# A hybrid decoder block on one core: an unnormalised first input projection, and two request orders changed

## The chip, the cores and the metric

The kernel runs on 1 core of one Trainium2 chip. The metric is the device time of one execution in microseconds (us). All engines named here belong to that core: PE (TensorE) multiplies matrices, DVE (VectorE), ACT (ScalarE) and POOL (GpSimd) work element by element, SP (SyncE) issues DMAs here.

## The reference

One decoder layer on 2048 tokens of width 1024, in f32. What matters of it here:

```
h = rmsnorm(x, norm_mix_gain)                 # x * rsqrt(mean(x*x) + eps) * gain
z = h @ w_in                                  # 1024 -> 3072, split into nine streams
y = [rglru(z...), hgrn2(z...), shortconv(z...)]     # three causal token mixers
x = x + y @ w_out
x = x + (silu(g) * u) @ w_down                # g, u = split(causal_conv3(rmsnorm(x) @ w_up))
x = x + sigmoid(x @ w_gate) * (p @ w_proj)
return rmsnorm(x, final_norm_gain)
```

The norm of a token is one number, 1/rms, which multiplies every feature of that token. So the product of a row of x (with the gain) and w_in, multiplied by 1/rms afterwards, is the same as the product of the normed row and w_in.

## The kernel before, in words

**Layout.** Features lie on the 128 partitions, tokens on the free axis. The 2048 tokens are worked in two halves (`hf`) of 1024, each in two chunks (`c`) of 512. A product in f32 is three matmuls (`mm3`, lines 265 to 267): both operands are split into a rounded part hi and a rest lo (`split`: hi by ACT, line 258; lo by a subtraction on DVE, line 259), and hi·hi, hi·lo and lo·hi are added in PSUM.

**Stages of a half.** The input projection (24 units of 128 columns in the order `IN_UNITS`; a unit is 2 chunks × 8 feature blocks × 3 = 48 matmuls of 128x512 into a PSUM tile `pz`) runs woven with the mixers; then come the output projection, the MLP (22 pairs of a gate block and an up block), the gate of the layer embedding, and the final norm of the half.

**Who sets the order.** The program is one long instruction stream in Python, and a scheduler gives each engine a fixed queue. On PE the mixers' small matmuls stand among the input projection's: a generator `G` of the projection's matmul triples is advanced by `fill(n)` (n triples, each one feature block of one chunk), `fill_to` and `weave`. When a unit is done, `evac` (line 559) calls the stream's function (`hg_f`, `hg_q`, `rg_u`, ...), which reads `pz` from PSUM. There are two tiles `pz`; a third unit can begin when the first one's readers are done. Weights are loaded by SP into three raw buffers `wr` and split in the order of a list (`w_upto`, `w_get` with a lookahead).

**The start.** SP loads x of chunk 0 (four tiles `xl` of 512 KB), constants, the first weights and x of chunk 1. The norm of a chunk (`Norm`) is 8 squares on ACT (line 306), 7 additions on DVE or POOL (line 308), 4 small matmuls `pm` (line 316), a few tiny steps on DVE and ACT (lines 319 to 325) and a broadcast `pr` by matmul (line 332). `h_apply` (line 416) then makes the normed h: `hx` = x * gain * 1/rms (line 420, DVE, reading `pr`) and a split. Only then can the first `pz` matmul run. The first two units are interleaved by chunk: unit 1 chunk 0, unit 2 chunk 0, unit 1 chunk 1, unit 2 chunk 1.

**The MLP's first pairs.** Pairs 0 and 1 go through `up_first`, later ones through `up(j)` in a scheme of seven quarter products (X[1] to X[7] are sums and differences of h, made in steps of the generator `h2`; the weights' sums `s` are made on DVE, lines 166 to 177, and split into `wt`). In `up(2)`, the third pair, PE first runs `pa` = X[1] times weight (1, hf, 2). Behind it stand the products into `pb`, `pa`, `pc`, and then the down projection `pdn` of pairs 0 and 1, which reads the activations `ahi` and `alo` that `gu_split` makes after `g_silu` and `gu_mul`. During the first half's MLP `stats_steps` loads x of the second half in pieces `xs` and squares and adds them, one piece per pair.

Of the kernel before, what the change touches and what calls it, by code (L numbers as in the profile page):

```python
# [9 lines left out]
F32 = mybir.dt.float32  # L10
F32R = mybir.dt.float32r
# [9 lines left out]
CH = 512  # L21
# [27 lines left out]
def trunk(ctx, tc, xT, pT, w_in, w_out, w_up, w_down, w_pp, w_pg, wr_bd, wi_bd, vecs, consts, masks, out):  # L49
# [34 lines left out]
    def ps2(name="ps2"):  # L84
        return mm.tile([P, TH], F32, tag="mm", name=nm(name))
# [4 lines left out]
    def cks(c):  # L90
        return slice(c * CH, (c + 1) * CH)
# [187 lines left out]
    def run(g):  # L279
        for _ in g:  # L280
            pass
# [134 lines left out]
    def h_apply(dst, xs, gain, pr, pool=()):  # L416

        for k in range(KD):
# [2 lines left out]
            dst[k] = split_chunk(s, "h", nc.gpsimd if k in pool else None)  # L421
            yield

    def stats_stream(hf, c):
        n = Norm()
        for k in range(KD):
            s = t2("xs")
            nc.gpsimd.dma_start(s, xT[k, :, hf * TH + c * CH : hf * TH + (c + 1) * CH])
            n.add(s)
        n.rstd()  # L430
        return n
# [8 lines left out]
    def x_load(xs, hf, c, eng):  # L440

        t0 = hf * TH + c * CH
        for k in range(0, KD, 2):
            t = t4("xl")
            eng.dma_start(t.rearrange("p (k t) -> p k t", k=2), xT[k : k + 2, :, t0 : t0 + CH].rearrange("k p t -> p k t"))
            xs += [t[:, :CH], t[:, CH:]]

    x_load(x0[0], 0, 0, nc.sync)
    nc.sync.dma_start(kt, consts[:, :KBLK])
    w_upto(1)  # L450
    nc.sync.dma_start(vt, vecs)
    w_upto(2)
    x_load(x0[1], 0, 1, nc.sync)
    norms = [Norm(), Norm()]
    for k in range(KD):
        norms[0].add(x0[0][k])
    norms[0].rstd()
    pr = norms[0].bcast()
    for k in range(KD):
        norms[1].add(x0[1][k], nc.gpsimd, True)  # L460
    run(h_apply(h[0], x0[0], "g1", pr))
    nc.vector.memset(hcar, 0.0)
    nc.vector.memset(scar, 0.0)

    for hf in range(NH):
# [91 lines left out]
        EVAC = [(9, hg_f), (6, hg_q), (12, hg_v), (15, hg_g), (0, rg_u), (3, rg_g), (20, sc_c), (22, sc_v), (18, sc_b)]  # L557

        def evac(m, ps):
            for b0, fn in EVAC:  # L560
                if b0 <= m < b0 + (3 if b0 < 18 else 2):
                    fn(m - b0, ps)

        done = [0]

        def gemm():

            ws, pss = [w_get("in", hf, m) for m in IN_UNITS[:2]], [ps2("pz"), ps2("pz")]
            for c in range(NC):
                for i in range(2):  # L570
                    yield from proj_gen(pss[i][:, cks(c)], ws[i], h[c])
                    if c == NC - 1:
                        evac(IN_UNITS[i], pss[i])
                        done[0] += 1
            for m in IN_UNITS[2:]:
                w, ps = w_get("in", hf, m), ps2("pz")
                for c in range(NC):
                    yield from proj_gen(ps[:, cks(c)], w, h[c])
                evac(m, ps)
                done[0] += 1  # L580

        G = gemm()
# [142 lines left out]
                ys[c][k] = split_chunk(y[k][:, cks(c)], "ys")  # L725

        if first:
            fill(6)
            norms[1].rstd()
            fill(5)  # L730
            run(h_apply(h[1], x0[1], "g1", norms[1].bcast(), (1, 3, 5)))
            with tc.issue_after(last_split[0].ins), tc.issue_after(last_split[1].ins):
                derived()
            t = t4("blk")[:, :P]
            nc.scalar.dma_start(t, consts[:, KBLK:])
            ACT(blk, t, AF.Copy)
# [137 lines left out]
        def gu_split(j):  # L874
            hi, lo = t4("ahi", F32R), t4("alo", F32R)
            split(hi, lo, zs[j, "g"])
            acts[j] = (hi, lo)

        def up_first():

            pairs = range(FIRST)
            w = {}
            sums0 = [[ps1(name="pa"), ps1(name="pa")], None]
            for j in pairs:
                zs[j, 0], zs[j, 1] = ftile("zg"), ftile("zu")
            for j in pairs:
                if j:
                    t = ps2("pbc")
                    sums0[j] = [t[:, C0], t[:, C1]]
                for i in range(2):  # L890
                    w[j, i] = w_get("f", hf, j, i)
                    prod(sums0[j][i], w[j, i], X[1], True, False)
                    ACT(zs[j, i][:, C1], sums0[j][i], AF.Copy)
                    if j == 0 and i == 0:
                        norms[1].rstd()
                    if j == 0 and i == 1:
                        h2 = h2_second(norms[1].bcast())
                        next(h2)
            for j in pairs:
                for i in range(2):  # L900
                    w[j, 2 + i] = w_get("f", hf, j, 2 + i, ahead=min(2, 3 - 2 * j - i))
                    prod(sums0[j][i], w[j, 2 + i], X[2], False, True)
                    ACT(zs[j, i][:, C0], sums0[j][i], AF.Copy)
                next(h2)

            sums1 = []
            for j in pairs:
                t = ps2("pbc")
                sums1.append([t[:, C0], t[:, C1]])
                for i in range(2):  # L910
                    prod(sums1[j][i], w[j, i], X[5], True, False)
            next(h2)
            for j in pairs:
                for i in range(2):
                    prod(sums1[j][i], w[j, 2 + i], X[3], False, True)
                    TT(zs[j, i][:, C1], zs[j, i][:, C1], sums1[j][i], op=ADD)
                if j == 0:
                    g_conv(0)
                    u_conv(0)
                    g_silu(0)  # L920
                    gu_mul(0)
                    gu_split(0)
                    run(h2)
                else:
                    g_conv(1)

        banks = {}

# [5 lines left out]
        def up(j):  # L934
            A, B = ps1(name="pa"), ps1(name="pb")
            banks[j] = A
            zg, zu = zs[j, 0], zs[j, 1] = ftile("zg"), ftile("zu")
            prod(A, w_mlp(1, hf, j), X[1], True, False)
            ACT(zg[:, C0], A, AF.Copy)
            if j % 2 == 0 or j == NJ - 1:  # L940
                g_silu(j - 1)
            prod(B, w_mlp(5, hf, j), X[5], True, False)
            ACT(zu[:, C1], B, AF.Copy)
            if j > FIRST:
                last_prod(j - 1)
            u_conv(j - 1)
            prod(A, w_mlp(6, hf, j), X[6], False, False)
            ACT(zg[:, C1], A, AF.Copy)
            gu_mul(j - 1)
            Cc = ps1(name="pc")  # L950
            prod(Cc, w_mlp(2, hf, j), X[2], True, True)
            TT(zg[:, C0], zg[:, C0], Cc, op=ADD)
            gu_split(j - 1)
            prod(B, w_mlp(3, hf, j), X[3], False, True)
            TT(zg[:, C1], zg[:, C1], B, op=ADD)
            prod(A, w_mlp(7, hf, j), X[7], False, False)
            TT(zu[:, C1], zu[:, C1], A, op=ADD)
            g_conv(j)
# [61 lines left out]
        stats = iter(()) if last else stats_steps()  # L1020
        for j in range(FIRST, NJ):
            up(j)
            next(stats, None)
            if j % 2 == 0 and j < NJ - 2:
                down_pair(j // 2 - 1, lambda: g_silu(j))
        run(stats)
# [167 lines left out]
```

## Time and profile before

| | |
|---|---|
| median of 3 runs | 2505.47 us (2500.73 to 2506.73) |
| the profiled execution's own time | 2501.25 us |
| its span | 2499.5 us |
| PE busy | 2423.0 us (97%) |
| DVE busy | 1578.3 us (63%) |
| ACT busy | 1253.3 us (50%) |
| POOL busy | 192.2 us (8%) |

The span is the traced part of the profiled execution. Busy time is the time in which an engine worked on data. An engine at 97% can only lose the time in which it waits or runs at a lower clock, or get fewer instructions.

### The profile page before, as it was taken

The page shows a single profiled execution, that of the slowest core. Times are in us where ns is not written, and L with a number is a line of the kernel's source. Part 1 is how long each engine was busy: PE and PEld are TensorE (multiplying, and loading weights), DVE is VectorE, ACT ScalarE, POOL GpSimd, SP SyncE. Part 2 cuts the span into 40 slices and gives each one's busy share as a digit, 9 for nine tenths or more (in the row PEclk, how much of TensorE's full clock was granted, in tenths as well). Part 3 has the DMA queues.
Part 4 walks back from the last instruction along what each step waited for, and adds up shares of the span by engine and source line. Part 5 has one row for each costly group of instructions (what it writes and reads, how often), then busy time and mean ns, then how long its engine had stood idle before and what let it go on. Part 6 is the DMA issues. An engine that isn't in the chain of part 4 may idle for free.

```text
span 2499.5 us, 33974 instructions
## 1 busy us (share of the span) xinstructions
PE 2423.0 (97%) x13660; PEld 1991.4 (80%) x13660; DVE 1578.3 (63%) x2396; ACT 1253.3 (50%) x1696; POOL 192.2 (8%) x240
## 2 busy tenths in 40 slices
PE   5999999889999999999999999998999999999998
PEld 4787788668888888888887787886888888888888
DVE  6566555585555565587565756567666666666856
ACT  5244873355555555545343457734555555555443
POOL 2000001001111111100110000010111111111000
PEclk9999999999999999999999999999999999999999
DMA  3101115435555555533431111251555555555442
GB/s 138 44 28 38 46 54 175 132 95 137 136 135 131 137 136 141 128 137 118 139 105 35 36 35 55 80 189 43 127 132 138 130 127 127 132 134 122 144 144 93
DMA packets 116542, 271.84 MB, mean 109 GB/s; under 512 B 11552, under 2 KB 39840, under 8 KB 116384
## 3 DMA queue, kind: packets, MB, share of 16 engines
q0 software_dynamic: 29056, 104.87, 19.9%
q1 hardware_dynamic: 86320, 163.78, 19.9%
q8 instruction: 107, 1.75, 0.3%
q10 hardware_dynamic: 1008, 1.02, 0.2%
q14 instruction: 51, 0.42, 0.1%
HBM read 177.34 MB, written 92.27 MB: 108 GB/s over the span
## 4 chain that ended last, share of the span: by engine, by line
PE 70%; DVE 4%; ACT 4%; issue 3%; DMA 2%; POOL 0%; SPq 0%; DVEq 0%; ACTq 0%; POOLq 0%
PE pdn L265 6%; PE pdn L267 6%; PE pdn L266 6%; PE pa L265 6%; PE pa L266 6%; PE pa L267 6%; PE pb L267 3%; PE pb L266 3%; PE pb L265 3%; PE pz L265 3%; PE pz L267 2%; PE pz L266 2%; PE pgt L265 2%; PE pgt L267 2%; PE pgt L266 2%
## 5 line engine op out<-in xcount | busy, mean ns | idle before, releaser
L265 PE MATMUL pz<-h,wh 128*128 128x512 f32 x768 | 306.8, 400 | 9.6 <-ACT h L258 9.6
L266 PE MATMUL pz<-h,wh 128*128 128x512 f32 x768 | 301.9, 394 | 2.0 <-DVE h L259 1.7
L267 PE MATMUL pz<-h,wl 128*128 128x512 f32 x768 | 300.7, 392 | 0.0
L265 PE MATMUL pa<-h,wt 128*128 128x512 f32 x672 | 265.1, 395 | 14.3 <-ACT wt L258 14.1
L265 PE MATMUL pdn<-ahi,wt 128*128 128x512 f32 x704 | 274.5, 390 | 1.3 <-ACT st L976 1.3
L267 PE MATMUL pdn<-ahi,wt 128*128 128x512 f32 x704 | 273.9, 389 | 0.0
L266 PE MATMUL pdn<-alo,wt 128*128 128x512 f32 x704 | 273.9, 389 | 0.0
L266 PE MATMUL pa<-h,wt 128*128 128x512 f32 x672 | 264.2, 393 | 0.0
L267 PE MATMUL pa<-h,wt 128*128 128x512 f32 x672 | 263.3, 392 | 0.2 <-DVE wt L259 0.2
L976 ACT ACTIVATE st<-pdn 128x1024 f32<-128x1024 f32 x144 | 147.8, 1027 | 193.6 <-PE pdn L267 182.1
L259 DVE TENSOR_TENSOR wt<-s,wt 128x512 fp32r<-128x512 f32 x160 | 108.4, 688 | 192.1 <-ACT wt L258 192.0
L977 POOL DMA_DIRECT2D xd<-st x144 | 123.2, 855 | 1035.1 <-ACT st L976 1034.4
L265 PEld LDWEIGHTS pz<-h,wh 128*128 128x128 f32 x768 | 145.0, 189 | 41.2 <-ACT h L258 10.7
L266 PEld LDWEIGHTS pz<-h,wh 128*128 128x128 f32 x768 | 145.2, 189 | 34.2 <-DVE h L259 4.6
L267 PEld LDWEIGHTS pz<-h,wl 128*128 128x128 f32 x768 | 145.2, 189 | 30.0
L259 DVE TENSOR_TENSOR wl<-wr,wh 128x1024 fp32r<-128x1024 f32 x120 | 146.2, 1226 | 34.1 <-ACT wh L258 34.0
L265 PEld LDWEIGHTS pa<-h,wt 128*128 128x128 f32 x672 | 127.6, 190 | 42.9 <-ACT wt L258 15.6
L265 PEld LDWEIGHTS pdn<-ahi,wt 128*128 128x128 f32 x704 | 132.1, 188 | 29.7 <-ACT st L976 2.5
L267 PEld LDWEIGHTS pdn<-ahi,wt 128*128 128x128 f32 x704 | 132.1, 188 | 27.7
L266 PEld LDWEIGHTS pdn<-alo,wt 128*128 128x128 f32 x704 | 132.2, 188 | 27.3
L267 PEld LDWEIGHTS pa<-h,wt 128*128 128x128 f32 x672 | 127.5, 190 | 28.4 <-DVE wt L259 1.7
L266 PEld LDWEIGHTS pa<-h,wt 128*128 128x128 f32 x672 | 127.7, 190 | 26.4
(273 smaller groups left out, 5058.6 us busy)
## 6 DMA issues: line engine op xcount, KB each, us to landing
xd<-st POOLq DMA_DIRECT2D x144, 512.0 KB, 6.3
wr<-in_w_up SPq DMA_DIRECT2D x176, 256.0 KB, 4.2
wr<-in_w_in SPq DMA_DIRECT2D x48, 512.0 KB, 3.5
q<-in_w_down SPq DMA_DIRECT2D x88, 256.0 KB, 3.4
wr<-in_w_pg SPq DMA_DIRECT2D x40, 512.0 KB, 4.4
wr<-in_w_out SPq DMA_DIRECT2D x32, 512.0 KB, 3.6
q<-in_w_up SPq DMA_DIRECT2D x40, 256.0 KB, 3.1
xr<-in_xT POOLq DMA_DIRECT2D x32, 256.0 KB, 4.0
```

The lines of the kernel that those rows point to most:

```text
L259: last_split[:] = i, (eng or nc.vector).tensor_tensor(lo, src, hi.bitcast(F32), op=SUB)
L265: MM(ps, wk[0], rk[0], start=start, stop=False, **kw)
L266: MM(ps, wk[0], rk[1], start=False, stop=False, **kw)
L267: MM(ps, wk[1], rk[0], start=False, stop=stop, **kw)
L976: ACT(st, ps, AF.Copy)
L977: nc.gpsimd.dma_start(xd[m], st, accum_op=ADD)
```

## The change

**At the start.** The queue of SP begins with the vectors, three weights and the constants, then x of both chunks. `h_raw` makes the operands of the first half's projection without a norm: hi = x * gain on ACT, lo = x * gain - hi in one DVE instruction. The norms' squares and additions are requested after the first two triples of the projection, and their small matmuls are placed between its triples by `fill`. 1/rms is copied from PSUM into an SBUF tile `rn`, and in the first half every unit's result is multiplied by it: two additional DVE products of 128x512 per unit, 48 in all, into a tile `zr`, which the stream's function reads in place of PSUM. `h_apply` with its 16 `hx`, 3 splits on POOL and 7 additions on POOL are gone from the first half. There the first three units run chunk by chunk (chunk 0 of all three, then chunk 1). In the second half the first two units are no longer interleaved.

**At the third pair.** `up_first` makes the weights (1, hf, 2) and (5, hf, 2) before the convolutions of pair 0. The silu, product and split of pair 0 and the last two steps of `h2` are kept in a list and requested one by one inside `up(2)`. `stats_steps` begins at pair 4.

```diff
+    def h_raw(dst, xs, gain, ks):
+        for k in ks:
+            t = dst[k] = t4("h", F32R)
+            ACT(t[:, :CH], xs[k], AF.Copy, scale=vec(gain, k))
+            STT(t[:, CH:], xs[k], vec(gain, k), t[:, :CH].bitcast(F32), op0=MUL, op1=SUB)
...
+    nc.sync.dma_start(vt, vecs)
+    w_upto(1)
     x_load(x0[0], 0, 0, nc.sync)
-    nc.sync.dma_start(kt, consts[:, :KBLK])
-    w_upto(1)
-    nc.sync.dma_start(vt, vecs)
     w_upto(2)
     x_load(x0[1], 0, 1, nc.sync)
+    nc.sync.dma_start(kt, consts[:, :KBLK])
     norms = [Norm(), Norm()]
-    for k in range(KD):
-        norms[0].add(x0[0][k])
-    norms[0].rstd()
-    pr = norms[0].bcast()
-    for k in range(KD):
-        norms[1].add(x0[1][k], nc.gpsimd, True)
-    run(h_apply(h[0], x0[0], "g1", pr))
+    h_raw(h[0], x0[0], "g1", range(KD))
+    w_upto(3)
+    h_raw(h[1], x0[1], "g1", range(KD))
...
         def evac(m, ps):
+            if first:
+                t = t4("zr")
+                for c in range(NC):
+                    TT(t[:, cks(c)], ps[c], rn[:, cks(c)], op=MUL)
+                ps = t
             for b0, fn in EVAC:
...
+                n = 3
+                ws = [w_get("in", hf, m, ahead=1) for m in IN_UNITS[:n]]
+                pss = [ps2("pz"), ps2("pz")]
+                pss = [[t[:, cks(c)] for c in range(NC)] for t in pss] + [[ps1(name="pz"), ps1(name="pz")]]
+                for c in range(NC):
+                    for i in range(n):
+                        yield from proj_gen(pss[i][c], ws[i], h[c])
...
         if first:
-            fill(6)
-            norms[1].rstd()
-            fill(5)
-            run(h_apply(h[1], x0[1], "g1", norms[1].bcast(), (1, 3, 5)))
+            rn = t4("rn")
+            fill(2)
+            for c in range(NC):
+                for k in range(KD):
+                    norms[c].add(x0[c][k], None, True)
+            for c, q in enumerate((23, 7)):
+                fill(q)
+                norms[c].rstd()
+                fill(3)
+                ACT(rn[:, cks(c)], norms[c].bcast(), AF.Copy)
...
                 if j == 0:
+                    w_upto(wat[5, hf, FIRST] + 1)
                     g_conv(0)
                     u_conv(0)
-                    g_silu(0)
-                    gu_mul(0)
-                    gu_split(0)
-                    run(h2)
                 else:
                     g_conv(1)
+
+            early.extend([lambda: g_silu(0), lambda: next(h2, None), lambda: gu_mul(0), lambda: gu_split(0), lambda: next(h2, None)])
...
         for j in range(FIRST, NJ):
             up(j)
-            next(stats, None)
+            if j > 3:
+                next(stats, None)
```

SP's queue at the start of the program, before; `xl` are the tiles of x, two feature blocks of one chunk each, `wr` raw weights, `kt` constants, `vt` vectors:

```order
L445 DMA xl_89<-in_xT 128x2x512
L445 DMA xl_91<-in_xT 128x2x512
L445 DMA xl_93<-in_xT 128x2x512
L445 DMA xl_95<-in_xT 128x2x512
L449 DMA kt<-in_consts 128x129
L112 DMA wr_98<-in_w_in 128x1024
L451 DMA vt<-in_vecs 128x197
L112 DMA wr_105<-in_w_in 128x1024
L112 DMA wr_232<-in_w_in 128x1024
L112 DMA wr_238<-in_w_in 128x1024
L445 DMA xl_111<-in_xT 128x2x512
L445 DMA xl_113<-in_xT 128x2x512
```

The same place after the change:

```order
L457 DMA vt<-in_vecs 128x197
L112 DMA wr_90<-in_w_in 128x1024
L112 DMA wr_104<-in_w_in 128x1024
L462 DMA kt<-in_consts 128x129
L112 DMA wr_143<-in_w_in 128x1024
L452 DMA xl_96<-in_xT 128x2x512
L452 DMA xl_98<-in_xT 128x2x512
L452 DMA xl_100<-in_xT 128x2x512
L452 DMA xl_102<-in_xT 128x2x512
L452 DMA xl_110<-in_xT 128x2x512
```

The first tile of x stood first and now stands behind the vectors, three weights and the constants; the four tiles of chunk 1 stand directly behind those of chunk 0, where three weights stood between.

ACT's queue at the third pair of the first half's MLP, before; `gu` are the activations of the pairs' convolutions, `h` parts of X, `wt` weights of pair 2 and later:

```order
L865 ACT_TABLE_LOAD
L865 ACTIVATE gu_4200<-gu_4200 128x1024
L406 ACTIVATE gu_4205<-zu_3899,vt 128x1024
L406 ACTIVATE gu_4258<-zg_3900,vt 128x1024
L306 ACTIVATE sq_6228<-xs_6226 128x512
L306 ACTIVATE sq_6523<-xs_6521 128x512
L258 ACTIVATE ahi_4212<-gu_4200 128x1024
L258 ACTIVATE h_4217<-h_487_3653 128x512
L258 ACTIVATE h_4221<-h_487_3653 128x512
L258 ACTIVATE h_4225<-h_488_3654 128x512
L258 ACTIVATE h_4229<-h_488_3654 128x512
L258 ACTIVATE wt_4270<-wr_4267 128x512
L258 ACTIVATE wt_4279<-s_4276 128x512
```

The same work after the change:

```order
L258 ACTIVATE wt_4247<-wr_4244 128x512
L258 ACTIVATE wt_4256<-s_4253 128x512
L258 ACTIVATE wt_4304<-s_4253 128x512
L258 ACTIVATE wt_4307<-wr_4250 128x512
L258 ACTIVATE wt_4328<-s_4253 128x512
L258 ACTIVATE h_4346<-h_497_3697 128x512
L406 ACTIVATE gu_4259<-zg_3942,vt 128x1024
L258 ACTIVATE h_4350<-h_497_3697 128x512
L258 ACTIVATE h_4354<-h_498_3698 128x512
L406 ACTIVATE gu_4264<-zu_3943,vt 128x1024
L887 ACT_TABLE_LOAD
L887 ACTIVATE gu_4259<-gu_4259 128x1024
```

The `wt` splits stood behind the silu of pair 0, its `ahi` and the four `h`; five of them now stand ahead of the convolutions' first taps, the silu and its table load, and `ahi` has moved ten rows behind the silu, out of this piece.

DVE's queue at the evacuation of the first units after the change (L568 are the products by 1/rms; `v` is the norm's tiny chain of chunk 1, `f`, `K` and `T` the first stream's tiles); before, the rows L489, L490 and L499 stood here without any L568:

```order
L325 TENSOR_TENSOR v_368<-v_368 128x4
L568 TENSOR_TENSOR zr_445<-pz_189,rn_182 128x512
L494 TENSOR_SCALAR f_448<-f_448,ms 128x1024
L495 TENSOR_SCALAR K_449<-f_448 128x1024
L504 TENSOR_TENSOR T_453<-f_448 128x512
L568 TENSOR_TENSOR zr_460<-pz_190,rn_182 128x512
L504 TENSOR_TENSOR T_453<-T_453 128x256
L568 TENSOR_TENSOR zr_460<-pz_190,rn_182 128x512
L504 TENSOR_TENSOR T_453<-T_453 128x128
```

Each unit's stream function now stands behind two products, and the second unit's stand within the first one's chain.

## Rows read from the trace of the kernel before

**Rows 1.** The page's first part: busy time, share and instructions of each engine.

```profile
PE 2423.0 (97%) x13660; PEld 1991.4 (80%) x13660; DVE 1578.3 (63%) x2396; ACT 1253.3 (50%) x1696; POOL 192.2 (8%) x240
```

**Rows 2.** Waits of PE over the whole run: total us, times, longest us.

```profile
PE pm L316 <- DVE sq L308: 16.8, 4, 11.7
PE pa L265 <- ACT wt L258: 14.1, 3, 8.0
PE pz L265 <- ACT h L258: 9.6, 3, 8.4
```

**Rows 3.** Busy time by stretch (engines' us and instructions, PEclk, DMA share, GB/s).

```profile
0.00:75.00 75.00, 49.44 (x198) 38.11 (x199) 51.92 (x110) 36.59 (x56) 15.84 (x15) 0.98 0.35 122
75.00:410.00 335.00, 330.20 (x2844) 266.14 (x2843) 198.50 (x311) 177.90 (x219) 5.03 (x9) 1.00 0.17 54
```

**Rows 4.** Timeline of PE, start of the program.

```profile
11.74 1.87 PE L316 MATMUL pm<-kt,sq 128*128 128x1 f32 x8 [11.74 <-DVE sq L308]
...
26.36 0.79 PE L265 MATMUL pz<-h,wh 128*128 128x512 f32 x1 [8.40 <-ACT h L258]
...
28.40 0.63 PE L267 MATMUL pz<-h,wl 128*128 128x512 f32 x1
28.82 0.63 PE L265 MATMUL pz<-h,wh 128*128 128x512 f32 x1
```

**Rows 5.** Timeline of ACT, start of the program and third unit's evacuation.

```profile
5.01 1.15 ACT L306 ACTIVATE sq<-xl 128x512 f32<-128x512 f32 x2 [2.30 <-DMA xl<-in_xT]
6.36 1.15 ACT L306 ACTIVATE sq<-xl 128x512 f32<-128x512 f32 x2 [0.20 <-DMA xl<-in_xT]
...
70.39 1.03 ACT L522 ACTIVATE v<-pz 128x1024 f32<-128x1024 f32 x1 [0.62 <-PE pz L267]
```

**Rows 6.** Groups by form on DVE: times | busy us, mean ns | idle.

```profile
L420 DVE SCALAR_TENSOR_TENSOR hx<-xl,vt,pr 128x512 f32<-128x512 f32 x32 | 22.5, 739 | 4.1 <-PE pr L332 4.1
...
L762 DVE TENSOR_TENSOR x<-xr,po 128x512 f32<-128x512 f32 x32 | 22.0, 687 | 73.2 <-PE po L267 45.4 <-DMA xr<-in_xT 27.8
...
L259 DVE TENSOR_TENSOR dp<-dv,dp 128x512 fp32r<-128x512 f32 x12 | 7.7, 684 | 0.0
```

**Rows 7.** Timeline of PE and POOL at the second half's first input unit.

```profile
1267.61 0.48 PE L265 MATMUL pz<-h,wh 128*128 128x512 f32 x1
...
1278.09 1.29 POOL L259 TENSOR_TENSOR h<-hx,h 128x512 fp32r<-128x512 f32 x1 [0.90 <-ACT h L258]
```

**Rows 8.** Timeline of PE, third pair of the first half's MLP.

```profile
519.34 0.39 PE L267 MATMUL pbc<-h,wt 128*128 128x512 f32 x1
...
527.72 0.80 PE L265 MATMUL pa<-h,wt 128*128 128x512 f32 x1 [7.99 <-ACT wt L258]
...
533.40 0.40 PE L267 MATMUL pa<-h,wt 128*128 128x512 f32 x1
...
547.06 0.39 PE L265 MATMUL pdn<-ahi,wt 128*128 128x512 f32 x1
```

**Rows 9.** Timelines of ACT (two rows) and DVE (one) around the same pair.

```profile
524.01 1.06 ACT L258 ACTIVATE ahi<-gu 128x1024 fp32r<-128x1024 f32 x1 [2.96 <-DVE gu L872]
...
527.06 0.61 ACT L258 ACTIVATE wt<-wr 128x512 fp32r<-128x512 f32 x1
...
543.60 1.23 DVE L259 TENSOR_TENSOR alo<-gu,ahi 128x1024 fp32r<-128x1024 f32 x1
```

**Rows 10.** Busy time of the stretches that end in the first pdn of each half.

```profile
480.00:547.00 67.00, 54.71 (x216) 42.89 (x216) 61.26 (x93) 39.44 (x62) 0.00 (x0) 0.90 0.25 80
1710.00:1767.00 57.00, 49.87 (x208) 39.14 (x208) 51.83 (x80) 31.43 (x48) 0.00 (x0) 0.97 0.13 42
```

**Rows 11.** Timeline of PE, third pair of the second half's MLP.

```profile
1743.09 0.39 PE L267 MATMUL pbc<-h,wt 128*128 128x512 f32 x1
...
1749.07 0.80 PE L265 MATMUL pa<-h,wt 128*128 128x512 f32 x1 [5.60 <-ACT wt L258]
...
1767.33 0.39 PE L265 MATMUL pdn<-ahi,wt 128*128 128x512 f32 x1
```

More of the change, by code (lines that the diff above doesn't have):

```diff
@@ L566, in gemm @@
         def gemm():
[L568 to L575, printed above, removed]
+            n = 0
+            if first:
+                n = 3
[5 more added lines that the diff above has]
+                        yield from proj_gen(pss[i][c], ws[i], h[c])
+                        if c == NC - 1 and i:
+                            for u in ([0, 1] if i == 1 else [i]):
+                                evac(IN_UNITS[u], pss[u])
+                                done[0] += 1
+            for m in IN_UNITS[n:]:
                 w, ps = w_get("in", hf, m), ps2("pz")
@@ L578, in gemm @@
                     yield from proj_gen(ps[:, cks(c)], w, h[c])
-                evac(m, ps)
+                evac(m, [ps[:, cks(c)] for c in range(NC)] if first else ps)
                 done[0] += 1
@@ L877, in gu_split, with later @@
             acts[j] = (hi, lo)
+        early = []
+        def later():
+            if early:
+                early.pop(0)()
         def up_first():
@@ L941, in up @@
                 g_silu(j - 1)
+            later()
             prod(B, w_mlp(5, hf, j), X[5], True, False)
+            later()
             ACT(zu[:, C1], B, AF.Copy)
@@ L948, in up @@
             ACT(zg[:, C1], A, AF.Copy)
+            later()
             gu_mul(j - 1)
@@ L952, in up @@
             TT(zg[:, C0], zg[:, C0], Cc, op=ADD)
+            later()
             gu_split(j - 1)
+            later()
             prod(B, w_mlp(3, hf, j), X[3], False, True)
```

## The prediction

> **What bounds the kernel now.** I read the page's first part first, to see which engine could be the limit: PE is busy for 2423.0 of the span's 2499.5 us, the next engine, DVE, for 63% [rows 1]. The change takes no product away, so on PE it can only win from the 76.5 us in which PE idles and from matmuls at a low clock. The waits of PE come next, since they say where these 76.5 us are. Three entries hold more than half: `pm` for a square's sum 16.8 us (11.7 of them once), `pa` for a weight split 14.1 (8.0 once), `pz` for an h 9.6 (8.4 once) [rows 2]. The stretches show that the start is the sparse place: PE is busy for 49.44 of the first 75 us, and then for 330.20 of 335, while the mixers run [rows 3]. So the kernel is PE-bound with two holes that the change aims at, the start and the third pair of each half's MLP. The timelines show what each hole consists of.
>
> At the start PE does nothing until 11.74 us, runs eight small `pm`, and has its first `pz` matmul only at 26.36, after a last wait of 8.40 us for h. Its first matmuls then come at 0.42 us spacing (28.40 to 28.82) [rows 4]. Full speed is 0.2275 us: 60 matmuls between 533.40 and 547.06 [rows 8]. The third unit is done just before 70.39 [rows 5].
>
> At the third pair PE's last matmul of pair 1 starts at 519.34, and `pa` at 527.72 [rows 8]. It waits for the split `wt` at 527.06, which stands on ACT behind `ahi` at 524.01, and that had waited 2.96 us for DVE's product `gu` [rows 9]. So the work of pair 0 holds the weight of pair 2 only because it stands ahead of it. The second half has the same hole, 1743.09 to 1749.07 [rows 11].
>
> **The change part by part.**
>
> *Start.* Before, the path was x, squares, sums, `pm`, `pr`, `hx`, split, matmul. After, it is x, one ACT copy, matmul. But x is loaded later. Tiles of x arrive 1.35 us apart (5.01, 6.36) [rows 5]; three weights of the same 512 KB, vectors and constants (0.17 MB) now go first, 3.3 tiles or 4.5 us. That puts the first x at about 9.4 us, chunk 0's last at 13.5 and chunk 1's last at 18.9. The first matmul follows one split later, about 10.3. Unit 1's chunk 0 is paced by x: its last block needs two DVE instructions of 0.74 [rows 6] after 13.5, and the unit-chunk ends at about 16.1. From there the rest of three units, 120 matmuls at 0.2275, takes 27.3 us. Two `pm` and two `pr` groups come between; the one in the rows takes 1.87 at a low clock [rows 4], I take 4.5 for the four. The first `pm` is placed after 75 matmuls, at 16.1 + 51 x 0.2275 = 27.7. Its squares can start on ACT only when both chunks are split (about 20), and the last addition ends at about 29: 1.3 us of wait. Unit 3 then ends at 16.1 + 27.3 + 4.5 + 1.3 = 49.2, against 70.4 before: 21.2 us ahead. I take off 2.0 for matmuls at the low pace after the first idle stretch (none, to some 20 x 0.19 = 4), and 1.5 for squares that may wait for a free tile (0 to 3). **Lead 17.7 us, bounds 14.2 to 21.2.** The additions that leave POOL (7) go to DVE, which loses 16 `hx` of 0.74 [rows 6] in exchange, so DVE is no fuller there.
>
> *The multiplication by 1/rms.* 48 products of 128x512 from PSUM. No row has this very form; the nearest is `x<-xr,po`, which also reads PSUM: 687 ns, and an SBUF split of that size takes 684 [rows 6]. That is 33.0 us of DVE, 27.5 of them for the 20 units in the mixer stretch, where DVE is busy for 198.50 of 335 us (59%) [rows 3]; it would be 226 (67%). What hides them is PE's own 10.9 us per unit (48 x 0.2275); if this cover were gone, all 27.5 would lie on the path. PE idles only 4.8 us there now, with DVE at 59%. That row is nearer to nothing than to the whole, so I take 3, bounds 0 and 14.
>
> The Trainium skill speaks against this step: its page "Perfetto Trace Analysis", section "Optimizing Scalar/DVE Operations", gives a DVE instruction about 60 ns of access overhead on SBUF and about 125 on PSUM. By it the 48 reads of PSUM would cost an estimated 3.1 us more of DVE, and the total would be at most 3.1 us later. The trace doesn't bear that out: 687 against 684 ns [rows 6].
>
> *Second half without interleaving.* Its first `pz` starts at 1267.61, and the last h of chunk 1, on POOL, starts at 1278.09 and ends at 1279.4 [rows 7]. Chunk 1 is now needed after 24 matmuls (5.5 us) instead of 48 (10.9), but its eight blocks are eaten one per 0.68 us, the last at about 1278.8. I take 0.5, bounds 0 and 1. **The projection's part is 17.7 - 3 - 0.5 = 14.2 us.**
>
> *Third pair.* With `wt` split before the convolutions of pair 0, PE can go on from 519.34. Six products of 12 matmuls stand before `pdn`: 519.57 + 72 x 0.2275 = 535.95 instead of 547.06, that is 11.1 us, 8.0 of wait and 3.1 of low-pace matmuls. In the second half it is 1743.32 + 16.4 = 1759.7 instead of 1767.33: 7.6 us. But what was late is still to be made: `alo` of pair 1, made at 543.60 before [rows 9], is next in line for `pdn`, and DVE is full there: 61.26 of 67 us, and 51.83 of 57 in the second half [rows 10]. The first half's stretch holds additions of `stats_steps`, which now begin at pair 4 (about 5 us of DVE at the 0.69 of [rows 6], for eight of them); with the idle 5.7 that makes room for 11. I take 10 there, bounds 5.7 and 11.1. The second half has no such additions and 5.2 us of DVE idle, plus the 2 us between the end of `alo` and `pdn`: I take 6.5, bounds 3 and 7.6. The statistics' later begin costs nothing: one piece per pair still fits in 18 pairs, and their ACT and DVE work lies beside the later pairs' matmuls. **Part: 16.5 us.**
>
> *Sum.* 14.2 + 16.5 = 30.7 us, 2501.25 - 30.7 = 2470.5 in the profiled execution's own time. The median shown is 4.2 above that execution, so medians may come out 0 to 4 higher; I give 2471.
>
> **The rivals.**
>
> *A: the multiplication's load falls half on PE.* For: DVE's queue is in order, a `zr` stands behind whatever mixer chain was requested before it, and the small matmuls of the chains wait for DVE. Against: 67% is no full engine. Price 14 instead of 3: 2481.5.
>
> *B: the hole at the third pair only moves to `pdn`.* For: the full DVE of [rows 10]. Against: several of its instructions there are for later weights, and can stand behind `alo`. The part gives 5.7 + 3 instead of 16.5: 2478.
>
> *C, the other side: slower.* The two `pz` tiles are released by `zr` products, which wait in DVE's queue; before, mostly ACT released them 1.03 us after the last matmul [rows 5]. If `zr` came more than a unit's time late in each unit, PE would stand at every third unit's begin. It decides when the 20 units wait more than (14.2 + 3 + 16.5) / 20 = 1.7 us each; with 2.2 us each the time is 2501.25 - 33.7 + 44 = 2512. Against: it needs DVE to be over 10.9 us behind in nearly every unit, with a third of its time free.
>
> *D: x comes late.* Every microsecond that x is later than 9.4 comes off the lead. If the whole lead goes, the start gives nothing and loses the 3 and 0.5: 2501.25 - 16.5 + 3.5 = 2488. Against: the spacing of [rows 5] is steady.
>
> **How the numbers follow.** Forecast 0.60, A 0.15, B 0.13, D 0.05, C 0.04, no change by something unseen 0.03. The forecast's own bounds: best 21.2 + 18.7 gives 2461; for its middle, 2463 to 2478. A and B lie within 2490, both together reach 2489. So the range is 2460 to 2490; C and the worst of D are left out. 0.3% is 7.5 us, about what a measurement of this kernel can tell from no change. Slower by over that is C and a little more, 0.05; within it 0.04; faster 0.91.
>
> **What would show it.** Right: first `pz` at 10 to 11 us, `v<-pz` of unit 3 at about 52 instead of 70.39; PE idle in the mixer stretch up by a few us; no wait of `pa` above 1 us at either third pair; `pdn` at about 16 to 17 us after pair 1's last matmul. Wrong: waits of `pz` for DVE `zr` at each unit (A, C); a wait of `pdn` for `alo` of several us (B); first `pz` after 12 us (D).

## The result and the profile after

The changed kernel takes 2473.34 us (median of 4 runs, 2470.63 to 2475.96), the kernel before beside it 2503.34 (4 runs): a ratio of 0.9886, with a 95% interval of 0.9871 to 0.9901. Forecast were 2471, and a range of 2460 to 2490. Timed again beside the experiments the ratio was 0.9883 (0.9869 to 0.9897). The gain of 29 to 30 us is real and has the forecast size; its parts have not.

The profiled execution of the changed kernel took 2475.96 us, the slowest of the four, so its 25.3 us of difference in span are less than the medians show (30.0). The page's first part and the waits of PE (total us, times, longest us), which answer to [rows 1, 2]:

```profile
PE 2419.0 (98%) x13660; PEld 1989.2 (80%) x13660; DVE 1597.7 (65%) x2438; ACT 1255.8 (51%) x1700; POOL 177.3 (7%) x230
```

```profile
PE pz L265 <- ACT h L428: 11.8, 1, 11.8
PE pmh L354 <- ACT sqp L258: 6.2, 4, 2.3
PE pdn L265 <- ACT st L1008: 5.1, 4, 2.4
PE pm L316 <- DVE sq L308: 4.2, 3, 2.4
...
PE pa L265 <- ACT wt L258: 0.5, 1, 0.5
```

The wait of `pa` for `wt` fell from 14.1 to 0.5 us, `pm` from 16.8 to 4.2. In exchange `pmh` (the norm of the mixers' results) and `pdn` (the down projection) wait more; neither was in the forecast's sum. The same two rows before:

```profile
PE pmh L354 <- ACT sqp L258: 4.5, 3, 2.0
...
PE pdn L265 <- ACT st L976: 1.3, 1, 1.3
```

ACT's first instructions (two weights' splits, then the copies of x), and PE's first; they answer to [rows 4, 5]:

```profile
5.82 1.06 ACT L258 ACTIVATE wh<-wr 128x1024 fp32r<-128x1024 f32 x1 [3.15 <-DMA wr<-in_w_in]
7.62 1.06 ACT L258 ACTIVATE wh<-wr 128x1024 fp32r<-128x1024 f32 x1 [0.74 <-DMA wr<-in_w_in]
10.99 5.34 ACT L428 ACTIVATE h<-xl,vt 128x512 fp32r<-128x512 f32 x8 [2.31 <-DMA xl<-in_xT]
```

```profile
11.76 0.79 PE L265 MATMUL pz<-h,wh 128*128 128x512 f32 x1 [11.76 <-ACT h L428]
...
13.57 0.63 PE L265 MATMUL pz<-h,wh 128*128 128x512 f32 x1
14.00 0.63 PE L266 MATMUL pz<-h,wh 128*128 128x512 f32 x1
...
31.09 0.95 PE L316 MATMUL pm<-kt,sq 128*128 128x1 f32 x8
```

The first `pz` comes at 11.76 and not at 10.3, because x is at hand at 10.99 and not at 9.4: the second weight came 1.8 us behind the first (5.82 to 7.62), and the constants, the third weight and the first tile of x took 3.4 us more (to 10.99), where the forecast had 1.35 us a tile. From there on the trace has the landings 1.35 us apart again: 10.90, 12.26, 13.60 and 14.97 for the four tiles of chunk 0. The eight copies then run nearly without a pause (5.34 us). After some low-pace matmuls (13.57 to 14.00, 0.43 us) PE runs without a wait until `pm` at 31.09, which has none either.

The stretches that answer to [rows 3, 10], and the new products' row. The last two end in the first `pdn` of a half, as in [rows 10], and hold the same count of PE's matmuls (216, and 210 for 208):

```profile
0.00:75.00 75.00, 62.10 (x323) 50.70 (x324) 53.98 (x121) 41.09 (x61) 1.15 (x5) 0.98 0.38 131
75.00:410.00 335.00, 328.60 (x2766) 264.74 (x2765) 222.20 (x349) 181.80 (x223) 6.08 (x11) 0.99 0.18 58
465.00:519.30 54.30, 51.19 (x216) 41.33 (x216) 52.20 (x79) 32.31 (x50) 0.00 (x0) 0.97 0.19 59
1691.50:1740.00 48.50, 47.95 (x210) 38.90 (x209) 47.51 (x75) 29.43 (x45) 0.00 (x0) 1.00 0.15 49
```

```profile
L568 DVE TENSOR_TENSOR zr<-pz,rn 128x512 f32<-128x512 f32 x48 | 31.6, 684 | 19.8 <-PE pz L267 16.7 <-ACT rn L753 3.0
```

PE is busy for 62.10 of the first 75 us (49.44 before). DVE in the stretch from 75 to 410 is at 66% (67% forecast). What PE did in 67 and 57 us ahead of the first `pdn` it now does in 54.3 and 48.5, and it is busy for 51.19 and 47.95 of them.

**Where the time goes, stage by stage.** Each figure is the start of the same record of PE in a kernel's trace minus that of the kernel before (for unit 3: the 144th `pz` record; "norm" is the last `pr` of the second norm of a half; the last line is the span). E1, E2, ... are the experiments below; E5 is the changed kernel profiled again. Single profiles differ by some us where nothing was changed: E2 leaves all ahead of the first MLP as it was and stands at -5.1 there.

| us against the kernel before | changed | E5 (same) | E1 start alone | E2 third pair alone | E3 no products |
|---|---|---|---|---|---|
| first `pz` (26.36 before) | -14.6 | -14.8 | -15.3 | 0.1 | -15.3 |
| unit 3 done | -19.6 | -19.8 | -20.2 | -1.7 | -20.2 |
| last `pz`, first half | -18.0 | -18.5 | -18.6 | -1.6 | -20.1 |
| last `po`, first half | -11.1 | -11.5 | -11.9 | -3.6 | -21.6 |
| norm, first half | -15.1 | -15.7 | -16.2 | -5.1 | -23.4 |
| first `pdn`, first half | -27.7 | -28.5 | -16.2 | -17.6 | -35.9 |
| last `pdn`, first half | -17.1 | -21.5 | -16.2 | -10.3 | -26.4 |
| first `pz`, second half | -17.1 | -21.5 | -16.2 | -10.3 | -26.4 |
| norm, second half | -18.5 | -22.8 | -17.4 | -11.2 | -27.8 |
| last `pdn`, second half | -27.3 | -31.6 | -17.0 | -19.9 | -36.3 |
| span | -25.3 | -31.9 | -17.0 | -20.2 | -36.2 |

### The profile page after: what moved, and what is told of

It reads as the page before. It is cut to its first block, busy times and chain, and to the rows that moved or that the text cites. A ratio compares the mean times of both kernels' runs of the same rounds, so it can differ in the third digit from the quotient of the medians.

```text
span 2474.2 us, 34028 instructions
## 1 busy us (share of the span) xinstructions
PE 2419.0 (98%) x13660; PEld 1989.2 (80%) x13660; DVE 1597.7 (65%) x2438; ACT 1255.8 (51%) x1700; POOL 177.3 (7%) x230
## 3 DMA queue, kind: packets, MB, share of 16 engines
q1 hardware_dynamic: 86320, 163.78, 20.2%
q0 software_dynamic: 29056, 104.87, 20.1%
## 4 chain that ended last, share of the span: by engine, by line
PE 55%; issue 18%; ACT 4%; DVE 3%; POOL 2%; DMA 1%; POOLq 0%; DVEq 0%; ACTq 0%
PE pdn L266 4%; PE pdn L265 4%; PE pdn L267 4%; PE pa L265 4%; PE pa L266 4%; PE pa L267 4%; PE pgt L265 2%; PE pgt L266 2%; PE pgt L267 2%; PE pz L265 2%; PE pz L267 2%; PE pz L266 2%; PE pb L266 2%; PE pb L267 2%; PE pb L265 2%
## 5 line engine op out<-in xcount | busy, mean ns | idle before, releaser
L266 PEld LDWEIGHTS pdn<-alo,wt 128*128 128x128 f32 x704 | 132.6, 188 | 28.5 <-DVE alo L259 1.3
L267 PEld LDWEIGHTS pa<-h,wt 128*128 128x128 f32 x672 | 126.3, 188 | 26.4
```

The costliest lines, as they stand in the source:

```text
L266: MM(ps, wk[0], rk[1], start=False, stop=False, **kw)
L267: MM(ps, wk[1], rk[0], start=False, stop=stop, **kw)
```

## The experiments

My theory after the trace: the two parts are independent; the start leads by 20 us, of which the products by 1/rms take back some 8, not spread over the mixers but at one place, their end; the third pair gives its share in both halves. All ratios are to the kernel before on the same chip (2497.6 to 2500.5 us there).

**E1, E2: each part alone.**

```diff
 E1 (from the changed kernel): up_first, up(j) and the start of stats_steps as before
 E2 (from the kernel before): up_first, up(j) and the start of stats_steps as changed
```

> Only the start's part (raw projection, products by 1/rms, the weights' order and the second half's order); the third pair as before. The prediction's sum gave this part 14.2 us: 2489 against 2503 before. The trace of the changed kernel reads otherwise: 19.6 us ahead when unit 3 is done, 18.0 at the end of the input projection, and about 8 of them given back at the begin of the output projection, which leaves some 10 to 11: 2492. Rival: the lead is lost altogether later on, because other waits take it up: 2500 or more.

> Only the third pair's part and the later statistics, in the kernel before. The prediction's sum gave 16.5 us: 2487. By the trace of the changed kernel it is 7 in the first half and 9.5 in the second: 2487 as well. Rival B of the prediction (the hole moves to the down projection): 8.7 us, 2495. If the two parts are independent, the savings of this run and of the run with the start alone add up to the whole, 30 us.

E1: 2485.4 us, ratio 0.9947 (0.9932 to 0.9962), 13 us. E2: 2482.8 us, ratio 0.9935 (0.9919 to 0.9952), 16 us. Together 1.2%, the whole 1.14 to 1.17%: the parts add. Forecast were 14.2 and 16.5, and E1 came out between the two expectations. PE's timeline in E1 has the old hole in both halves, unchanged, which shows that only the second part removes it:

```profile
511.54 0.79 PE L265 MATMUL pa<-h,wt 128*128 128x512 f32 x1 [7.99 <-ACT wt L258]
...
1731.65 0.80 PE L265 MATMUL pa<-h,wt 128*128 128x512 f32 x1 [5.60 <-ACT wt L258]
```

**E3, E8: no products, and twice as many.**

```diff
 E3
         def evac(m, ps):
-            if first:
+            if first and m == IN_UNITS[2]:
                 t = t4("zr")
 E8
                     TT(t[:, cks(c)], ps[c], rn[:, cks(c)], op=MUL)
+                    TT(t[:, cks(c)], t[:, cks(c)], rn[:, cks(c)], op=MUL)
```

> The changed kernel with 46 of the 48 products by 1/rms left out: the streams read the unnormalised results from PSUM (the third unit keeps its two). The norm's squares, sums and the tile rn are still made. Theory: the products cost some 1.6 us in the mixers and most of the 8 us at the begin of the output projection, where DVE's queue is late: about 9 us less than the changed kernel, 2464. Rival: the products are hidden and the late output projection is a matter of the order alone: 2473, as the changed kernel.

> The changed kernel with a second product by 1/rms on each result, in place in SBUF: 48 more DVE instructions of 0.68 us, 33 us of DVE (this changes the results). Leaving 46 products out moved the end of the output projection's norm by about 8 us. Theory: DVE's queue is not full but late at some places, so the price grows faster than linearly: 10 to 20 us more than the changed kernel. Rival C of the prediction, PE held at each unit: 30 us or more. Rival that the products are hidden: no more than 3.

E3 (which leaves 46 of the 48 products by 1/rms out): 2466.6 us, ratio 0.9871 (0.9851 to 0.9891). E8: 2475.1 us, ratio 0.9902 (0.9887 to 0.9917). By the ratios the products cost 3 to 4 us (0.9871 against 0.9883 and 0.9886), but the intervals overlap; the stages say it sharper. In E3 the lead of unit 3, 20.2 us, is still 20.1 at the last `pz` and 21.6 at the last `po`; with the products it falls to 18.0 and 11.1, 18.5 and 11.5, 18.6 and 11.9 in three kernels. So they take some 2 us in the mixers and 8 between the last `pz` and the last `po`; at the norm 7 to 8 of the 10 are left. In E8 33 us more of DVE work cost some 5 us (ratio 0.9902 against 0.9883 beside it) and 3 to 4 us at the norm (-11.9 against -15.1 to -16.2): my expectation of 10 to 20 fell. In the mixers E8's lead falls by 2.3 us, the changed kernel's by 1.2 to 1.6, so there the load on DVE is nearly hidden. Most of the price arises at one place, the mixers' end. The second products' row:

```profile
L569 DVE TENSOR_TENSOR zr<-zr,rn 128x512 f32<-128x512 f32 x48 | 31.8, 684 | 0.2
```

**What the delay is.** The split `ys` that the output projection waits for starts 15.0 us behind the last `pz` in the changed kernel, 6.8 us in E3. ACT's timeline of the changed kernel at the end of the first half's mixers, from the last squares' split on (L346 are the logarithms of the last norm, L348 its exponentials, L532 the silu of the last unit):

```profile
350.01 1.13 ACT L258 ACTIVATE sqp<-sqh 128x512 fp32r<-128x512 f32 x2
351.16 1.28 ACT L346 ACT_TABLE_LOAD   x1
354.14 0.69 ACT L346 ACTIVATE sqh<-pmh,epsc 128x512 f32<-128x512 f32 x1 [1.70 <-PE pmh L355]
354.85 1.28 ACT L348 ACT_TABLE_LOAD   x1
356.14 0.63 ACT L348 ACTIVATE sqh<-sqh 128x512 f32<-128x512 f32 x1
356.79 1.28 ACT L346 ACT_TABLE_LOAD   x1
358.09 0.69 ACT L346 ACTIVATE sqh<-pmh,epsc 128x512 f32<-128x512 f32 x1
358.79 1.28 ACT L532 ACT_TABLE_LOAD   x1
360.09 1.06 ACT L532 ACTIVATE sg<-zr 128x1024 f32<-128x1024 f32 x1
361.17 1.28 ACT L348 ACT_TABLE_LOAD   x1
362.46 0.63 ACT L348 ACTIVATE sqh<-sqh 128x512 f32<-128x512 f32 x1
363.00 0.61 ACT L258 ACTIVATE ys<-ysc 128x512 fp32r<-128x512 f32 x1
```

The same place in E3:

```profile
346.31 1.03 ACT L532 ACTIVATE sg<-pz 128x1024 f32<-128x1024 f32 x1 [1.41 <-PE pz L267]
347.35 1.28 ACT L346 ACT_TABLE_LOAD   x1
348.65 1.27 ACT L346 ACTIVATE sqh<-pmh,epsc 128x512 f32<-128x512 f32 x2
349.93 1.28 ACT L348 ACT_TABLE_LOAD   x1
351.23 1.15 ACT L348 ACTIVATE sqh<-sqh 128x512 f32<-128x512 f32 x2
352.68 1.30 ACT L258 ACTIVATE ys<-ysc 128x512 fp32r<-128x512 f32 x2 [0.30 <-DVE ysc L349]
```

Without the products the silu runs as soon as the last unit is done, then one table load serves both logarithms and one both exponentials: 4.0 us from the first logarithm to the split `ys` (348.65 to 352.68). With them the silu must wait for `zr`, the order becomes logarithm, exponential, logarithm, silu, exponential, and each change loads a table for 1.28 us: 8.9 us from the first logarithm to `ys` (354.14 to 363.00). That is 4.8 of the 8.2 us. The other 3.4 lie ahead of it: the first logarithm comes 6.2 us behind the last `pz`, 2.8 in E3, because the squares' split is late. DVE is busy there for 9.11 of the 10 us from 340 to 350 (5.12 in E3), with splits of the mixers' results that E3 makes from 330 on. PE stands at both ends of that chain, for the squares' split at its begin and for `ys` at its end:

```profile
350.67 1.32 PE L354 MATMUL pmh<-sqp,blk 128*128 128x512 f32 x2 [2.30 <-ACT sqp L258]
...
363.66 0.51 PE L265 MATMUL po<-ys,wh 128*128 128x512 f32 x1 [2.07 <-ACT ys L258]
```

Behind each wait PE runs at a lower pace: the granted clock is 0.66 from 350 to 355 and 0.74 from 365 to 370, that is partly at 1.2 and not 2.4 GHz, and 1.00 from 355 to 360. Each wait with the slow matmuls around it costs some 4 us.

ACT's table loads alone aren't the delay. In E8 both logarithms and both exponentials stand together, so there are three loads and not five, and yet it loses 7.8 us from the last `pz` (348.29) to the last `po`, more than the changed kernel's 6.9. Its first logarithm is later still, and its silu stands ahead of `ys`:

```profile
356.39 1.27 ACT L346 ACTIVATE sqh<-pmh,epsc 128x512 f32<-128x512 f32 x2 [2.69 <-PE pmh L355]
...
361.44 1.06 ACT L532 ACTIVATE sg<-zr 128x1024 f32<-128x1024 f32 x1
362.40 1.14 ACT L258 ACTIVATE ys<-ysc 128x512 fp32r<-128x512 f32 x2
```

The Trainium skill has a rule for the loads, on its page "ScalarE: Activation LUTs", section "Rules for kernel authors": several transcendental functions are to be grouped by table set, one set done before the next. The trace agrees: ungrouped there are 5 loads of 1.28 us here, where E3 and E8 have 3.

**E4, E6: mending that end.** E4 splits four of the mixers' results earlier; E6 adds two orders.

```diff
 E4
+        for k in order[:4]:
+            ysplit(k)
         weave(sc_chain(0), 23, 3)
-        for k in order[:6]:
+        for k in order[4:6]:
 E6, beside that
+            if first and m == IN_UNITS[-1] and not now:
+                late.append(lambda: evac(m, ps, True))     # run behind ysplit(7)
+                return
...
+            with tc.issue_after(ln.ins):                   # the second logarithm
+                ACT(sq[c], sq[c], AF.Exp, scale=-0.5)
```

> The changed kernel with the splits of four mixer results y (8 on ACT, 8 on DVE) requested before the last two short convolution chains and not between them. Theory: DVE's queue ends the mixers late, and these splits stand ahead of the last norm's squares there; without them PE's waits at the begin of the output projection (2.3 and 2.1 us, and the low pace after each) go: 4 to 7 us less than the changed kernel, 2467 to 2469. Rival: the waits are set by the last unit's own chain (product, silu, product, split), which this doesn't shorten: no more than 1 us.

> The changed kernel with three orders mended at the end of the first half's mixers: four results y split earlier (as in the run before), the last unit's product and silu requested behind the last norm, and both logarithms of a norm ahead of its exponentials (in both halves), so that ACT loads its tables for them once and not in turn. Theory: what is lost there is ACT's chain of table loads (five of 1.28 us between the norm's matmuls and the split that po waits for): the wait of 2.1 us goes, with the low pace behind it, 3 to 5 us less than the changed kernel. Rival: the wait only moves to the split of the last unit's result: no more than 1 us.

E4: 2471.6 us, ratio 0.9890 (0.9873 to 0.9906), no change: the first wait was still 2.41 us, so these splits don't set it, and no more than about 1 us was won, as the rival had it. E6: 2467.9 us, ratio 0.9880 (0.9865 to 0.9895), beside 0.9883 for the changed kernel. What the stages show is clearer than the total: from the last `pz` to the last `po` E6 loses 3.4 us against the kernel before, E4 5.7, the changed kernel 6.9 and 7.0. Its chain on ACT has one load for each function:

```profile
352.21 1.28 ACT L346 ACT_TABLE_LOAD   x1
353.86 1.39 ACT L346 ACTIVATE sqh<-pmh,epsc 128x512 f32<-128x512 f32 x2 [0.36 <-PE pmh L356]
355.26 1.28 ACT L349 ACT_TABLE_LOAD   x1
...
358.01 1.30 ACT L258 ACTIVATE ys<-ysc 128x512 fp32r<-128x512 f32 x2 [0.30 <-DVE ysc L350]
```

From the first logarithm to `ys` it takes 4.2 us (353.86 to 358.01), 8.9 in E4 and the changed kernel. E6 differs from E4 by two edits, the logarithms' place and the last unit's; together they win 2.3 us, about a third of the loss there. Which of the two does it, fewer table loads or the silu behind `ys`, wasn't parted, and the late squares remain (a wait of 2.40 us). As a gain of the total it isn't shown: the intervals overlap.

**E7, E9: x ahead of the second weight.**

```diff
 E7 and E9
     x_load(x0[0], 0, 0, nc.sync)
-    w_upto(2)
+    with tc.issue_after(last_x[0].ins):        # E9: behind h_raw(h[0]) on ACT as well
+        w_upto(2)
     x_load(x0[1], 0, 1, nc.sync)
...
-    w_upto(3)
+    with tc.issue_after(last_x[0].ins):
+        w_upto(3)
```

> The changed kernel with only one weight ahead of x in SP's queue; the second stands behind chunk 0, the third behind chunk 1. Theory: the start is bound by the first x tile's landing. Two tiles less ahead of it are 2.7 us; the first pz comes at 8.5 to 9.5 instead of 11 to 11.8, but unit 1 is then paced by x; unit 3 is done 2 to 3 us earlier, and the total is 2 to 3 us lower. Rival: the weights are then the late ones, units 2 and 3 wait, and nothing is won.

> As the run with x first, but the second weight's split now stands behind chunk 0's eight copies on ACT (there it stood ahead of them, and they waited for a weight that landed at 14.6 us). Theory: the start is bound by the first x, and ACT's order has to follow SP's; the first pz comes at 7.5 to 9 us instead of 11.1 to 11.8, unit 3 is done 3 to 4 us earlier than in the changed kernel, and the total is 2 to 4 us lower. Rival: unit 2 then waits for its weight's split, which stands behind the eight copies, and unit 3 is done no earlier.

Both were slower than the changed kernel, against what I expected: E7 2475.7 us (0.9907, 0.9894 to 0.9919; its runs, 2473.8 to 2476.2, lie above all of E5's on the same chip, 2467.8 to 2470.4), E9 2478.3 us (0.9917, 0.9904 to 0.9931). ACT's timelines say why, E7 first:

```profile
14.68 1.06 ACT L258 ACTIVATE wh<-wr 128x1024 fp32r<-128x1024 f32 x1 [7.48 <-DMA wr<-in_w_in]
```

```profile
19.99 1.06 ACT L258 ACTIVATE wh<-wr 128x1024 fp32r<-128x1024 f32 x1 [5.64 <-DMA wr<-in_w_in]
```

In E7 the second weight's split stands ahead of the copies of x in ACT's queue; with the weight now loaded later, ACT waits 7.48 us for it, though the first tile of x landed at 9.29, and the first `pz` is at 16.40. In E9 that is mended and the first `pz` is at 8.79; but the third weight's split still stands ahead of chunk 1's copies and waits 5.64 us. The squares behind them come late, PE waits 3.55 us for 1/rms at 45.88, and unit 3 is done 15.6 us earlier than before the change, where the changed kernel has 19.6 to 19.8 (E7: 14.4). A load that is moved must move with the instruction that waits for it, on each in-order engine.

**E10, E12: both ends.** E10 is E9 with E6's orders, and with 1/rms multiplied into y ahead of the two gate units of the short convolution; E12 also brings the loads into ACT's order.

```diff
 E10
             z["y", j] = yt
+            if first:
+                TT(yt, yt, rn, op=MUL)         # and no zr for units 18 and 19
 E12
     with tc.issue_after(last_x[0].ins), tc.issue_after(last_h[0].ins):
-        w_upto(2)
-    x_load(x0[1], 0, 1, nc.sync)
+        w_upto(3)
+    with tc.issue_after(last_w[0].ins):
+        x_load(x0[1], 0, 1, nc.sync)
```

> The run before joined with the three orders mended at the end of the mixers, and with one product moved off the last path: for the two units of the short convolution's first gate, y * (z * 1/rms) is computed as (y * 1/rms) * z, so that 1/rms is multiplied into y before the unit's matmuls are done. Theory: the two groups of savings add, 5 to 8 us less than the changed kernel, 2462 to 2465 beside 2470. Rival: the end of the mixers is again taken up by other waits, and only the start's 2 to 4 us are left.

> The run before last but one (start and end mended) with the third weight's load ahead of chunk 1 of x, as its split stands ahead of chunk 1's copies on ACT, and later weights behind chunk 1. Theory: in the two runs with x first ACT stood still for 5.6 us before chunk 1's copies, waiting for the third weight, and the squares, sums and 1/rms came later by that; with the loads in ACT's order the first pz stays at 8.4 to 8.8 us, the waits of pr (1.0 and 3.6 us) go, unit 3 is done 3 us earlier than in the changed kernel, and with the end of the mixers mended the total is 4 to 7 us below the changed kernel: a ratio of 0.986 to 0.987 to the kernel before, where the changed kernel has 0.988 to 0.989. Rival: the lead of the start is lost in the next queue again, and the ratio is that of the changed kernel.

E10: 2472.3 us, ratio 0.9888 (0.9875 to 0.9902): the end is partly mended (2.5 us lost from the last `pz` to the last `po`), but the start is E9's, with unit 3 done 15.0 us earlier. E12: 2469.0 us, ratio 0.9878 (0.9862 to 0.9895). The end of the mixers is mended in E12's trace (0.7 us lost from the last `pz` to the last `po`, instead of 7), but its start is no better: the first `pz` comes at 8.96, and unit 3 is done 17.2 us earlier than before the change. PE waits there for 1/rms:

```profile
45.08 2.05 PE L334 MATMUL pr<-kt,v 128*128 128x128 f32 x8 [2.97 <-DVE v L327]
```

The squares start on ACT at 22.39, hardly earlier than in the changed kernel (23.03), since chunk 1's copies stand ahead of them; PE, started earlier, only comes to `pr` too early. So once x is early, the norm's chain is the next bound of the start. No version is shown to beat the changed kernel; E12 and E6 have the lowest ratios by 0.0003 to 0.0008, which is inside the intervals.

**E5: the changed kernel again,** without an edit.

> The changed kernel once more, as the measure for the runs beside it on the same chip, and for a second profile: 28 to 30 us below the kernel before. Theory: its losses at the begin of the output projection stand in this profile too (waits of about 2.3 us of the norm's matmul and 2.1 us of po, with a low pace behind), since the queues' orders make them. Rival: they were an accident of the one profile, and are gone or elsewhere.

2469.6 us, ratio 0.9883 (0.9869 to 0.9897). The two waits stand in this profile too, at 350.15 (2.30 us) and 361.88 (2.06 us), and the stages of the table agree within 1 us up to the norm of the first half: the queues' orders make them.

**E11: the statistics from pair 2 again.**

```diff
             up(j)
-            if j > 3:
-                next(stats, None)
+            next(stats, None)
```

> The changed kernel with the statistics of the second half begun at pair 2 again. The prediction gave their delay a part in the third pair of the first half: DVE is full there, and eight additions less make room. Theory: with them back, the activations of pairs 0 and 1 come 3 to 5 us later and the down projection waits for them: 3 to 5 us more, in the first half only. Rival: the additions find other places, and the time is that of the changed kernel.

2472.7 us, ratio 0.9891 (0.9876 to 0.9906) beside 0.9883 and 0.9886 for the changed kernel: not told apart from it, and the first `pdn` comes 14.1 us behind the last `pbc` as there (520.16 and 506.10; 519.34 and 505.29). The delayed statistics are not shown to win anything.

## Why the prediction was right, step by step

**The start's lead** was forecast as 17.7 us and is 19.2 to 20.2 at unit 3 in the eight profiles that have this start (the changed kernel, E1, E3 to E6, E8, E11). Errors went against each other. The first `pz` was to come at 10.3 and came at 11.0 to 12.1, because the first tile of x landed later than 9.4 (10.90 in the changed kernel). This is rival D, 1.5 us of it, and yet the lead grew: the small matmuls `pm` and `pr` took 3.2 to 3.4 us and not 4.5, and the 2.8 us that were set down for waits of `pm` and for the squares didn't come. The low pace cost some 2 us, as taken.

**The multiplication by 1/rms** is the step that was mis-sized: 3 us were taken ("bounds 0 and 14"), and the stages show 7 to 8: some 2 in the mixers, the rest at their end. The forecast looked for what hides 27.5 us of DVE work, and PE's 10.9 us per unit do nearly hide it, as E8 shows. It overlooked that the last unit has no unit behind it: there the products make DVE's queue late and upset ACT's order on the way to the output projection. Rival A's price (14 instead of 3) is about as far off on the other side. Its mechanism, small matmuls that wait behind DVE's queue, is seen at that one place, in the waits of `pmh`, and not through the mixers. Rival C, PE held at every unit, is excluded by E8. The Trainium skill's figure that was weighed there (page "Perfetto Trace Analysis", section "Optimizing Scalar/DVE Operations": DVE dearer on PSUM) is not borne out: the products take 684 ns from PSUM, and E8's second ones 684 ns from SBUF.

**The second half without interleaving** was to cost 0.5 us. The stretch from its first `pz` to the norm differs by -0.7 to -1.4 in the nine profiles of kernels that drop the interleaving and haven't E6's orders, and by -0.9 in E2, which keeps it: nothing.

**The third pair** was to give 10 and 6.5 us. In the second half it gives 8.8 from the norm to the last `pdn` (8.8 in E5, 8.7 in E2; E1, which is without it, loses 0.5), more than the bound of 7.6. The bound counted the one hole alone; a wait of `pbc` for DVE's `zg`, 0.78 us at 1740.46 before, is gone too. DVE, which the forecast feared, is even fuller ahead of the first `pdn` than before, 47.51 of 48.5 us and 52.20 of 54.3, but PE's waits for `alo` come to 0.8 us in the whole run. The first `pdn` stands 14.1 us behind pair 1's last matmul in the first half and 12.2 in the second, not 16 to 17, since the first products into `pa` now run ahead of that matmul.

In the first half the hole is gone as well: at the first `pdn` the gain since the norm is 12.7 us (12.8 in E5, 12.5 in E2), more than the 10 of the forecast and its bound of 11.1. But 7 us of it are lost again within the next 80 us, in all three and in E11, and at the last `pdn` 2.1, 5.8 and 5.2 are left. The step of the forecast that was wrong here is that it took the lead at the first `pdn` for the gain. The largest loss is the down projection waiting for its own evacuation:

```profile
537.05 0.63 ACT L306 ACTIVATE sq<-xs 128x512 f32<-128x512 f32 x1 [3.32 <-DMA xs<-in_xT]
537.59 1.01 ACT L1008 ACTIVATE st<-pdn 128x1024 f32<-128x1024 f32 x1
...
558.89 0.63 ACT L306 ACTIVATE sq<-xs 128x512 f32<-128x512 f32 x1 [4.32 <-DMA xs<-in_xT]
```

```profile
538.65 0.80 PE L265 MATMUL pdn<-ahi,wt 128*128 128x512 f32 x1 [2.35 <-ACT st L1008]
...
583.36 0.50 PE L265 MATMUL pa<-h,wt 128*128 128x512 f32 x1 [1.39 <-ACT zg L977]
```

ACT stands 3.32 us at a square of the next half's statistics whose piece `xs` hasn't landed, and later 4.32 us at another; the copy `st` behind it frees the PSUM tile that `pdn` needs. With the slow matmuls around it this wait costs 4 us, where one of its kind cost 1.6 before. Two more short waits, `pa` for ACT's `zg` at 583.36 and `pdn` for `alo` at 588.40 (0.75 us), cost 3 us in the same count. This is rival B in its effect (part of the hole moves to `pdn`), with another cause: mostly not `alo`, but a DMA ahead of ACT's copy. The second half, which has no statistics to make, loses nothing behind its first `pdn` (-27.4 there, -27.3 at the last). That the squares are the cause was read from the traces and not tried by a run without them. Their later begin isn't: E11, which begins them at pair 2, loses the same 7 us, with waits of 0.82 and 1.52 us at this place. The changed kernel's own profile loses 3.5 us more near 900 us, with two waits of `pdn` for `st` (1.24 and 1.21 us), and E5's has none there, so that part differs between executions of one kernel.

**The sum**: forecast 14.2 + 16.5, measured alone 13 and 16, together 29 to 30. That each part came out is in part luck: in the start the larger lead made up for the products' delay, and at the third pair the second half made up for a part of what the first half lost.

## What to carry to other kernels

When work is moved from ahead of a long product to behind each of its parts, price the last part by itself: the others are hidden by their successor, the last one lies on the path to the next stage. The same holds for a hole that is closed: follow the lead past the place where it was, to the end of the stage. An added dependency also changes the order in which a scheduler takes its neighbours, and on ACT a changed order can mean a table load per instruction. A wait that is removed at PE shows the next thing in another engine's in-order queue; look there for instructions that wait for a DMA ahead of one that PE waits for.

## What the runs showed of the hardware

A load's place in the queue did not give its time. Before, the first four loads of 512 KB landed 1.34 to 1.39 us apart. After the change the first four (three weights and a tile of x, with 65 KB of constants between) landed at 5.80, 7.60, 9.05 and 10.90, up to 1.9 us apart, and those behind them, x and weights, 1.3 to 1.4 us apart. What makes the first ones slower was not tried. A DVE product of 128x512 takes 684 ns whether its operand lies in PSUM or in SBUF. And a change of table on ACT cost 1.28 us and no more here: the exponential at 356.14 follows the load at 354.85 directly.
